# A two-layer diffusion backbone on one core: operands at one address residue, a later spill, and conditioning sums finished in fours

## The chip, the cores and the metric

The kernel runs on one core of one Trainium2 chip. The metric is the device time of one execution in microseconds (us), the median of several runs. One further execution was recorded by the profiler; its times are the ones quoted from the trace.

The engines are TensorE (PE, with its weight loads PEld), VectorE (DVE), ScalarE (ACT), GpSimd (POOL) and SyncE (SP), whose queue issues nearly all DMAs of this kernel. SBUF has 128 partitions; all byte addresses below are addresses within a partition.

## The reference

512 latent tokens and 256 context tokens of width 1024 go through two layers. Layer 0 mixes tokens by centred mean pooling, layer 1 by grouped-query attention; each is followed by a squared-ReLU MLP of width 4096. Every sub-layer is normed before and after, and shift, scale and gate come from a conditioning vector by a linear map per layer:

```python
def ada_mods(cond, w, b):
    m = (jax.nn.silu(cond) @ w + b)[..., None, :]
    return jnp.split(m, N_MOD, axis=-1)

def sq_relu_mlp(h, w_in, w_out):
    return jnp.square(jax.nn.relu(h @ w_in)) @ w_out

def reference(x, c, ctx, c_ctx, ...):
    for i in range(DEPTH):
        last = i == DEPTH - 1
        sh1, sc1, gt1, sh2, sc2, gt2 = ada_mods(c, w_ada[i], b_ada[i])
        csh1, csc1, cgt1, csh2, csc2, cgt2 = ada_mods(c_ctx, w_ada[i], b_ada[i])
        h_lat = modulate(rms_norm(x, g_mix_pre[i]), sh1, sc1)
        ...
        x = x + gt1 * rms_norm(y_lat, g_mix_post[i])
        m_lat = sq_relu_mlp(modulate(rms_norm(x, g_mlp_pre[i]), sh2, sc2), w_mlp_in[i], w_mlp_out[i])
        x = x + gt2 * rms_norm(m_lat, g_mlp_post[i])
        if not last:
            ...
    return x
```

The context stream gets the same in layer 0, with the conditioning vector `c_ctx`; in layer 1 it serves only as keys and values. So the six modulation vectors of layer 0 and `SH1`, `SC1` of layer 1 are needed for two conditioning vectors, the others of layer 1 for one. All is in float32.

## The kernel before

**Split matmuls.** Each float32 operand is kept as two parts of a faster matmul format, `hi` (a rounded copy) and `lo` (the rest). A product is three matmuls: hi·hi + hi·lo + lo·hi. So every weight tile that lands from HBM (1 MB, 128 x 2048, a tile `raw`) is split: ScalarE copies `hi` (L120), VectorE subtracts to get `lo` (L123). `Ring.load` does the load and the split.

**Where the operands lie.** `ra` (normed activations for the input matmuls), `rb` (hidden activations and others) and the three slots `unit` for split weights are the operands of nearly all matmuls. `unit[0]` is a part of `rb` at first; `unit[1]` and `unit[2]` are the tile `units`, which is allocated after a small tile `phase` of 24 floats. Its start, 124768, is 352 modulo 512; `ra` and `rb` start at 416 modulo 512. The tile `sums` starts at 157600, 416 modulo 512, over the memory of the residual `xr`, which starts at 157632; so `xr` is spilled to DRAM before `sums` is written, and loaded again after the first MLP.

**Stages.** The start (0 to 110 us) loads inputs and layer 0's conditioning weights and does the pooling mixer. Then come the first MLP (110 to 610), norms and QKV (610 to 733), attention (733 to 830), its output product (830 to 909) and the second MLP (909 to 1248).

**The first MLP** goes over 16 groups g of 256 hidden columns with all 768 tokens. Group 0 is done by `Inner` (L526); from group 1 on, `Seven` (L636) does the input product of a group with seven half-size products instead of eight. For this `sums` holds sums of activations, and `weights_sums` makes sums of weights, with short VectorE steps of 128 x 512 (L610 to L615) and splits of 128 x 1024 (L602, L603). `out_mm` (L731) does the output product of a group; its moving operand is `w_out`, split in `unit[2]`, and `out_ev` (L740, L742) adds the result into `acc`. The weight buffers `raw` are three, shared with the conditioning weights. **The second MLP** does the same for 512 tokens without `Seven`; its weights go through four slots in turn, two in `units` and two in `ra`.

**Conditioning.** A unit is one 256-column piece of a modulation vector of layer i. The first 20 units (layer 0, all but `GT2`) are computed on TensorE at the start (`ada_mm`, L212, and `ada_sel`, L219). The other 28 run on VectorE during the first MLP, by `ada_sum`: the piece of `w_ada` is loaded, eight passes over 128 x 256 multiply it by the conditioning vector and add up (L246, L251; twice eight for two vectors), a transpose (L254) and a reduction (L256) into a small tile `part` follow. `ada_fin` then spreads the sums over the partitions by small matmuls (L219) and adds the bias (L229). `ada_step` is called twice in each group, by `extra0` before the group's input product and by `mid0` ahead of its seventh product: each call finishes the unit of one group before and sums a new one. Twelve units have two vectors, sixteen have one.

**What sets the order.** Code of the start, of the last group and of attention goes into a `Steps` object, `st.at(t, f, ...)`, which sorts it by hand-written due times. After that the framework's scheduler sets the order on each engine by its own estimate of time, except for what `keep_in_program_order` pins. So the order on an engine can change at places that the code leaves alone.

The allocations that fix the places are these:

```python
ra = const.tile([P, 2 * KT * TOK], F32R, name="ra")
rb = const.tile([P, 10240], F32R, name="rb")
phase = ctx.enter_context(tc.tile_pool(name="phase", bufs=1)).tile([P, 24], F32, name="phase")
...
units = ctx.enter_context(tc.tile_pool(name="units", bufs=1)).tile([P, 2 * 4096], F32R, name="units")
```

## Time and profile before

| | us |
|---|---|
| median of 3 runs | 1252.26 (1252.23 to 1252.82) |
| the profiled execution | 1250.13 |
| its span in the trace, first to last instruction | 1248.2 |
| busy: TensorE matmuls | 1191.6 |
| busy: VectorE | 923.5 |
| busy: ScalarE | 524.6 |
| mean granted TensorE clock | 0.985 |

Lines of the profile have the form "start, duration, engine, tiles, line, count" in the chain of waits (the chain of work that ended last, followed back from the end) and in the timeline. In the timeline and the wait rows the square bracket names the idle time before an instruction and what ended it, and `x24` says that 24 like instructions are joined in a row. A group row gives after the bar the total busy time and the mean in ns of one, then the idle time before the group. Matmuls are pipelined, so the mean of one (some 390 ns) is longer than the distance from one to the next (some 230 ns). A window row gives the stretch, its length, then for PE, PEld, DVE, ACT and POOL the busy time with the count, the granted clock, the share of DMA and its GB/s.

### The profile page before, as it was taken

To read this page: it belongs to the slowest core of one execution; us is meant where nothing else is said; L and a number is where in the kernel's file an instruction comes from. 1 tells how busy PE (TensorE), PEld (TensorE's weight loads), DVE (VectorE), ACT (ScalarE), POOL (GpSimd) and SP (SyncE) were. 2 spreads that over 40 slices of the span, in tenths; PEclk is the share of its full clock that TensorE was granted. 3 is DMA by queue.
4 is the path that set the end of the run, shared out by engine and by line. 5 is a ranking of instruction groups with operands and counts; after the bars stand their busy time and mean duration, and the time that the engine had idled before them with its cause. 6 is when DMAs were issued, how large, how long until landed. Compare 5 with 4: busy or idle time off the path is not lost.

```text
span 1248.2 us, 16629 instructions
## 1 busy us (share of the span) xinstructions
PE 1191.6 (95%) x6602; PEld 1017.9 (82%) x6602; DVE 923.5 (74%) x1546; ACT 524.6 (42%) x868; POOL 101.8 (8%) x135
## 2 busy tenths in 40 slices
PE   6889989999999999999999989999999999999997
PEld 5669878888888888888787879988878888888886
DVE  3877998999898999987687589872664554555555
ACT  5666313433333333333476358862632222313222
POOL 1060000000000000000242232001100000000001
PEclk9899989999999999999999989999999999999999
DMA  9985044444444444343521211020233242333201
GB/s 330 345 296 177 1 139 131 135 135 135 136 135 135 135 133 138 124 128 122 198 72 54 82 34 35 1 81 21 68 119 117 70 133 68 103 100 96 73 1 68
DMA packets 105006, 143.71 MB, mean 115 GB/s; under 512 B 2608, under 2 KB 88032, under 8 KB 104928
## 3 DMA queue, kind: packets, MB, share of 16 engines
q1 hardware_dynamic: 104928, 142.64, 35.0%
q8 instruction: 52, 0.85, 0.3%
q14 instruction: 26, 0.21, 0.1%
HBM read 137.39 MB, written 5.24 MB: 114 GB/s over the span
## 4 chain that ended last, share of the span: by engine, by line
PE 78%; DVE 9%; DMA 6%; ACT 3%; issue 1%; POOL 1%; SPq 1%; DVEq 0%; POOLq 0%; ACTq 0%
PE pso L731 30%; PE psin L636 16%; PE psin L526 14%; PE psq L851 5%; DMA raw<-in_w_ada 4%; PE psy L1090 3%; PE po L1064 3%; PE pss L1025 2%; DMA raw<-in_w_mlp_in 2%; PE pspt L1050 1%; ACT junk L146 1%; PE pspool L454 1%; DVE xr L310 1%; PE psada L212 1%; DVE units L123 1%
## 5 line engine op out<-in xcount | busy, mean ns | idle before, releaser
L731 PE MATMUL pso<-units,rb 128*128 128x512 f32 x1542 | 376.6, 396 | 1.9 <-DVE units L123 1.7
L731 PEld LDWEIGHTS pso<-units,rb 128*128 128x128 f32 x1542 | 289.2, 189 | 66.4 <-DVE units L123 2.0
L742 DVE TENSOR_TENSOR acc<-acc,pso 128x512 f32<-128x512 f32 (+1 forms) x281 | 183.7, 680 | 107.2 <-PE pso L731 107.1
L120 ACT CAST units<-raw 128x2048 fp32r<-128x2048 f32 (+1 forms) x46 | 72.7, 1597 | 116.8 <-PE pso L731 95.5
L251 DVE SCALAR_TENSOR_TENSOR rows<-raw,cond,rows 128x256 f32<-128x256 f32 x280 | 117.1, 480 | 0.0
L123 DVE TENSOR_TENSOR units<-raw,units 128x2048 fp32r<-128x2048 f32 (+1 forms) x44 | 86.2, 1972 | 28.1 <-ACT units L120 28.1
L731 PE MATMUL pso<-ra,rb 128*128 128x512 f32 (+1 forms) x390 | 91.1, 386 | 0.0
L157 POOL TENSOR_SCALAR ms<-ss 128x1 f32<-128x1 f32 x21 | 10.5, 502 | 973.2 <-ACT junk L146 972.6
L526 PE MATMUL psin<-ra,units 128*128 128x512 f32 (+1 forms) x320 | 87.5, 375 | 0.0
L731 PEld LDWEIGHTS pso<-ra,rb 128*128 128x128 f32 x390 | 72.6, 188 | 15.2
L526 PE MATMUL psin<-ra 128*128 128x512 f32 x256 | 80.3, 390 | 0.0
L120 ACT CAST ra<-raw 128x2048 fp32r<-128x2048 f32 x16 | 30.4, 1906 | 108.6 <-PE pso L731 82.8
L636 PE MATMUL psin<-ra,units 128*128 128x384 f32 x336 | 66.2, 342 | 1.2 <-ACT psin L648 0.6
L526 PEld LDWEIGHTS psin<-ra,units 128*128 128x128 f32 x320 | 58.7, 188 | 9.3
L636 PE MATMUL psin<-sums,units 128*128 128x384 f32 x336 | 65.4, 342 | 0.5 <-ACT psin L644 0.3
L636 PEld LDWEIGHTS psin<-ra,units 128*128 128x128 f32 x336 | 58.0, 188 | 4.7 <-ACT psin L648 3.2
L636 PEld LDWEIGHTS psin<-sums,units 128*128 128x128 f32 x336 | 57.7, 188 | 3.0 <-ACT psin L644 1.8
L526 PEld LDWEIGHTS psin<-ra 128*128 128x128 f32 x256 | 48.1, 188 | 10.3
L123 DVE TENSOR_TENSOR ra<-raw,ra 128x2048 fp32r<-128x2048 f32 x16 | 36.6, 2291 | 25.2 <-ACT ra L120 25.2
L851 PE MATMUL psq<-units,ra 128*128 128x512 f32 x216 | 53.0, 397 | 0.0
L659 ACT ACTIVATE work<-work 128x768 f32<-128x768 f32 x14 | 11.9, 847 | 91.5 <-DVE work L654 91.5
L526 PE MATMUL psin<-rb,ra 128*128 128x512 f32 x128 | 49.9, 390 | 0.0
(214 smaller groups left out, 2045.5 us busy)
## 6 DMA issues: line engine op xcount, KB each, us to landing
raw<-in_w_ada SPq DMA_DIRECT2D x48, 1024.0 KB, 7.7
raw<-in_w_mlp_in SPq DMA_DIRECT2D x32, 1024.0 KB, 5.5
raw<-in_w_mlp_out SPq DMA_DIRECT2D x32, 1024.0 KB, 5.0
raw<-in_w_qkv SPq DMA_DIRECT2D x6, 1024.0 KB, 5.3
raw<-in_w_o SPq DMA_DIRECT2D x4, 1024.0 KB, 5.1
spill<-xr SPq DMA_DIRECT2D x6, 512.0 KB, 10.5
xr<-spill SPq DMA_DIRECT2D x6, 512.0 KB, 6.9
xr<-in_x SPq DMA_DIRECT2D x4, 512.0 KB, 4.5
```

Of the source, the lines that this page charges most:

```text
L120: a = gp.tensor_copy(hi, raw) if pool_hi else sc.copy(hi, raw)
L123: b = (gp if pool_lo else ve).tensor_tensor(out=lo, in0=raw, in1=hi, op=ALU.subtract)
L146: sc.activation(junk[:, 0:src.shape[-1]], src, AF.Square, scale=float(D) ** -0.5, accum_out=ss)
L251: ve.scalar_tensor_tensor(out=r, in0=raw[:, k, :], scalar=cond[:, k, c:c + 1], in1=r, op0=ALU.mult, op1=ALU.add)
L526: te.matmul(ps[:, bank, o:o + ln], w[:, k, fs], rhs, start=(k == 0 and n == 0), stop=(k == KT - 1 and n == 2))
L636: te.matmul(bank, w[k], a[k], start=start and k == 0 and m == 0, stop=stop and k == 3 and m == 2, skip_group_check=True)
L731: te.matmul(pss[h][:, 0:cols[h][1]], a[:, f, ts_], w[:, f, cols[h][0]:sum(cols[h])], start=(n == 0), stop=(n == len(seq) - 1))
L742: ve.tensor_tensor(out=d, in0=d, in1=ps[:, 0:w], op=ALU.add)
L851: te.matmul(ps, a[:, k, sl], w[:, k % 4, :], start=(k == 0 and n == 0), stop=(k == KT - 1 and n == 2))
L1025: te.matmul(ps[:, c2, 0:384], a[:, sl], b[:, kv, 384 * c2:384 * c2 + 384], start=(n == 0), stop=(n == 2))
L1064: te.matmul(po[:, 0:256], v[:, kt, hs], p[:, kt, qs], start=(kt == 0 and n == 0), stop=(kt == NT - 1 and n == 2))
L1090: te.matmul(ps, a[:, k, sl], w[:, k % 4, o:o + width], start=(k == 0 and n == 0), stop=(k == KT - 1 and n == 2))
```

## The change

1. `phase` grows from 24 to 40 floats, 64 bytes. `units` then starts at 124832, 416 modulo 512, and so do all the matmul operands named above.
2. The six spills of the residual are issued in `sums()`, in program order behind group 1's `w_in` and group 0's `w_out`, instead of at due times in the start.
3. `ada_sum` writes its reduction into a tile `parts` of 192 floats, cut off the end of `sums`. `ada_fin` finishes the four units of one modulation vector at a time (four matmuls, one bias step), three steps after the fourth sum. No unit runs in group 0; 24 units run in groups 1 to 12, one with two vectors and one with one vector in each.
4. The four units of (layer 1, `GT2`) are summed in groups 4 to 7 of the second MLP and finished in its group 10; there `gate_diag` follows, which stood in the attention's output stage.
5. In the first MLP the weights that `Ring.load` splits are split in two halves of 1024 columns each.

```diff
-    phase = ctx.enter_context(tc.tile_pool(name="phase", bufs=1)).tile([P, 24], F32, name="phase")
+    phase = ctx.enter_context(tc.tile_pool(name="phase", bufs=1)).tile([P, 40], F32, name="phase")
...
+    def split_halves(raw, hi, lo):
+        for q in range(2):
+            z = slice(1024 * q, 1024 * q + 1024)
+            sc.copy(hi[:, z], raw[:, z])
+            ve.tensor_tensor(out=lo[:, z], in0=raw[:, z], in1=hi[:, z], op=ALU.subtract)
...
-            if wait is None:
+            if wait is None and self.halves:
+                split_halves(raw, hi, lo)
+            elif wait is None:
                 split(raw, hi, lo, pin)
...
-        s = small.tile([P, 2, 8], F32, tag="part", name="part", bufs=2)
-        ve.tensor_reduce(out=s[:, 0:nc_, :], in_=raw[:, 0:nc_, :].rearrange("p c (g q) -> p c g q", q=32),
-                         axis=AX.X, op=ALU.add)
-        rowsd[i, m, j] = s, nc_
-
-    def ada_fin(i, m, j):
-        part, nc_ = rowsd.pop((i, m, j))
+        ve.tensor_reduce(out=part.rearrange("p (c g) -> p c g", c=nc_),
+                         in_=raw[:, 0:nc_, :].rearrange("p c (g q) -> p c g q", q=32), axis=AX.X, op=ALU.add)
+
+    def ada_fin(i, m, parts, nc_):
+        n = 4 * nc_
         ps = psB.tile([P, 512], F32, tag="b", name="psada")
-        ada_turn(ps[:, 0:2 * nc_], part[:, 0:nc_, :].rearrange("p c (b a) -> p a c b", a=4), nc_)
-        ada_out(i, m, j, ps[:, 0:2 * nc_], nc_)
+        for a in range(4):
+            te.matmul(ps[32 * a:32 * a + 32, 0:2 * n], sel,
+                      parts.rearrange("p (u c b a) -> p a u b c", c=nc_, b=2, a=4)[:, a], start=True, stop=True)
+        ada_out(i, m, 0, ps[:, 0:2 * n], nc_, 8)
...
     def sums():
+        for t in (4, 5, 0, 1, 2, 3):
+            sy.dma_start(spill[:, t], xr[:, t])
         held.close()
...
-        f = S["held"].enter_context(tc.tile_pool(name="sums", bufs=1, side="right")).tile([P, 8712], F32R, name="sums")[:, 0:8704]
+        pool = S["held"].enter_context(tc.tile_pool(name="sums", bufs=1, side="right"))
+        f, parts[0] = pool.tile([P, 8520], F32R, name="sums"), pool.tile([P, 192], F32, name="parts")
...
-        st.at([61.98, 66.18, 70.38, 74.58, 78.78, 82.98][n], lambda t: sy.dma_start(spill[:, t], xr[:, t]), t)
...
-            one = lambda z: Ring([z])
+            one = lambda z: Ring([z], True)
...
-    def ada_step(slot, kinds):
-        for u in due[slot]:
-            ada_fin(*u[:3])
-        due[slot] = [kinds.pop(0)] if kinds else []
-        for u in due[slot]:
-            ada_sum(*u)
+    dual = [(0, GT2, 2), (1, SC1, 2), (1, SH1, 2)]
+    lone = [(1, m, 1) for m in (GT1, SC2, SH2)]
+    work, due = [], []
+    for n in range(12):
+        work.append((*dual[n // 4], n % 4, 64 * (n // 4 % 2)))
+        work.append((*lone[n // 4], n % 4, 128 + 32 * (n // 4 % 2)))
+
+    def ada_step():
+        for u in [u for u in due if u[0] <= 0]:
+            ada_fin(*u[1:])
+        due[:] = [(u[0] - 1, *u[1:]) for u in due if u[0] > 0]
+        if work:
+            i, m, nc_, j, at = work.pop(0)
+            ada_sum(i, m, j, nc_, parts[0][:, at + 8 * nc_ * j:at + 8 * nc_ * j + 8 * nc_])
+            if j == 3:
+                due.append((2, i, m, parts[0][:, at:at + 32 * nc_], nc_))
...
     def mid0(g):
-        ada_step(1, lone)
+        if g:
+            ada_step()
...
-        ada_step(0, dual or lone)
-        if g == NG - 2:
-            ada_step(1, [])
+        if g:
+            ada_step()
...
-        at(36, gate_diag, 1, GT2, 0, 1)
...
+    def extra1(g):
+        if g == 3:
+            slot[0:NL] = [1] * NL
+            parts[1] = small.tile([P, 32], F32, tag="part", name="part", bufs=1)
+        if 3 < g < 8:
+            ada_sum(1, GT2, g - 4, 1, parts[1][:, 8 * g - 32:8 * g - 24])
+        if g == 10:
+            ada_fin(1, GT2, parts[1], 1)
+            gate_diag(1, GT2, 0, 1)
```

**The DMA queue of SP in the start.** The first fence is the queue before, from the load of group 0's `w_in` (`raw<-in_w_mlp_in`) on; `in_w_ada` are conditioning weights, `spill<-xr` the spills.

```order
L106 DMA raw<-in_w_mlp_in 128x8x256
L703 DMA spill<-xr 128x1024
L106 DMA raw<-in_w_ada 128x8x256 x2
L703 DMA spill<-xr 128x1024
L106 DMA raw<-in_w_ada 128x8x256 x2
L703 DMA spill<-xr 128x1024
L106 DMA raw<-in_w_ada 128x8x256
L703 DMA spill<-xr 128x1024 x3
L106 DMA raw<-in_w_mlp_in 128x8x256
L106 DMA raw<-in_w_mlp_out 128x2x1024
L106 DMA raw<-in_w_ada 128x8x256 x2
```

The same stretch after the change:

```order
L106 DMA raw<-in_w_mlp_in 128x8x256
L106 DMA raw<-in_w_ada 128x8x256 x4
L571 DMA spill<-xr 128x1024 x2
L106 DMA raw<-in_w_ada 128x8x256
L571 DMA spill<-xr 128x1024 x3
L106 DMA raw<-in_w_mlp_in 128x8x256
L106 DMA raw<-in_w_mlp_out 128x2x1024
L571 DMA spill<-xr 128x1024
L106 DMA raw<-in_w_mlp_out 128x2x1024
L106 DMA raw<-in_w_mlp_in 128x8x256
L106 DMA raw<-in_w_ada 128x8x256 x2
```

Four of the five conditioning loads now stand ahead of every spill, the last spill stands behind the next two MLP weights, and the first conditioning loads of the MLP stand behind group 1's weights.

**TensorE between groups 0 and 1.** The 96 matmuls are the last of group 0's input product; `pso` is the output product, `psada` a finish of a conditioning unit, and `psin` of 128x384 behind it the products of `Seven`. Before:

```order
L526 MATMUL psin<-ra,units 128x384 x96
L731 MATMUL pso<-units,rb 128x512 x72
L219 MATMUL psada<-part,sel 32x2x2 x4
L219 MATMUL psada<-part,sel 32x2 x4
L731 MATMUL pso<-units,rb 128x512 x18
L636 MATMUL psin<-ra,units 128x384 x2
L731 MATMUL pso<-units,rb 128x512 x5
L636 MATMUL psin<-ra,units 128x384 x10
```

After:

```order
L534 MATMUL psin<-ra,units 128x384 x96
L741 MATMUL pso<-units,rb 128x512 x24
L647 MATMUL psin<-ra,units 128x384 x12
L741 MATMUL pso<-units,rb 128x512 x51
L647 MATMUL psin<-sums,units 128x384 x4
L741 MATMUL pso<-units,rb 128x512 x21
L647 MATMUL psin<-sums,units 128x384 x20
```

The two finishes between the output matmuls of groups 0 and 1 are gone, and 12 matmuls of the next input product stand among the 72 of group 0.

**VectorE ahead of the split of group 1's `w_out`** (`units<-raw,units`). `rows<-raw,cond,rows` is a pass of a conditioning sum, `acc<-pso` an evacuation of an output product, `work<-raw` a short step of the weights' sums. Before:

```order
L740 COPY acc<-pso 128x512
L251 SCALAR_TENSOR_TENSOR rows<-raw,cond,rows 128x256 x2
L740 COPY acc<-pso 128x512
L251 SCALAR_TENSOR_TENSOR rows<-raw,cond,rows 128x256
L740 COPY acc<-pso 128x512
L251 SCALAR_TENSOR_TENSOR rows<-raw,cond,rows 128x256 x3
L123 TENSOR_TENSOR units<-raw,units 128x2048
```

After:

```order
L626 TENSOR_TENSOR work<-raw,work 128x512
L121 TENSOR_TENSOR units<-raw,units 128x1024
L259 SCALAR_TENSOR_TENSOR rows<-raw,cond,rows 128x256
L121 TENSOR_TENSOR units<-raw,units 128x1024
L259 SCALAR_TENSOR_TENSOR rows<-raw,cond,rows 128x256
L614 TENSOR_TENSOR units<-work,units 128x1024
```

The split is now two halves, with short steps of the weights' sums ahead of it where passes of the conditioning sums stood.

More of the change, by code (lines that the diff above doesn't have):

```diff
@@ L129, in backbone, with __init__ @@
     class Ring:
-        def __init__(self, slots):
-            self.slots, self.n = slots, 0
+        def __init__(self, slots, halves=False):
+            self.slots, self.n, self.halves = slots, 0, halves
         def load(self, src, width, pin=False, wait=None):
@@ L225, in ada_sel, with ada_out @@
         ada_out(i, m, j, ps[:, 256:260], 2)
-    def ada_out(i, m, j, ps, nc_):
+    def ada_out(i, m, j, ps, nc_, w=2):
         at = m * KT + 2 * j
-        ve.tensor_tensor(out=mods[i][:, at:at + 2, 0:nc_], in0=ps.rearrange("p (b c) -> p b c", c=nc_),
-                         in1=cols[:, i * 48 + at: i * 48 + at + 2].unsqueeze(2).broadcast_to([P, 2, nc_]),
+        ve.tensor_tensor(out=mods[i][:, at:at + w, 0:nc_], in0=ps.rearrange("p (b c) -> p b c", c=nc_),
+                         in1=cols[:, i * 48 + at: i * 48 + at + w].unsqueeze(2).broadcast_to([P, w, nc_]),
                          op=ALU.add)
@@ L234, in ada_out, with ada_sum @@
             g0 = 96 + s * 16 + i * KT + 2 * j
-            ve.scalar_tensor_tensor(out=avec[i][s][:, 2 * j:2 * j + 2, 0:nc_], in0=mods[i][:, at:at + 2, 0:nc_],
+            ve.scalar_tensor_tensor(out=avec[i][s][:, 2 * j:2 * j + w, 0:nc_], in0=mods[i][:, at:at + w, 0:nc_],
                                     scalar=1.0,
-                                    in1=cols[:, g0:g0 + 2].unsqueeze(2).broadcast_to([P, 2, nc_]),
+                                    in1=cols[:, g0:g0 + w].unsqueeze(2).broadcast_to([P, w, nc_]),
                                     op0=ALU.add, op1=ALU.mult)
-    def ada_sum(i, m, j, nc_):
+    def ada_sum(i, m, j, nc_, part):
         raw = raw_load(w_ada[i, :, m * D + j * 256: m * D + (j + 1) * 256]
```

7 lines of the change are left out of this document (2 added, 5 removed).

## The prediction

> **What bounds the kernel now.** I read the head of the page first, then the windows by stage, the chain of work that ended last, and the timelines of the places that the change touches.
>
> ```profile
> PE 1191.6 (95%) x6602; PEld 1017.9 (82%) x6602; DVE 923.5 (74%) x1546; ACT 524.6 (42%) x868; POOL 101.8 (8%) x135
> PE 78%; DVE 9%; DMA 6%; ACT 3%; issue 1%; POOL 1%; SPq 1%; DVEq 0%; POOLq 0%; ACTq 0%
> 228.30:293.30 65.00, 64.85 (x351) 56.49 (x345) 61.19 (x121) 23.97 (x31) 0.00 (x0) 1.00 0.41 130
> 909.00:1219.00 310.00, 308.22 (x1344) 251.75 (x1343) 171.43 (x197) 86.76 (x86) 0.00 (x0) 1.00 0.27 89
> ```
>
> TensorE is busy 95% of the span and holds 78% of the chain. In the second MLP (909 to 1219 us) it is the only bound: 308 of 310 us busy, VectorE 171. In the first MLP (the window at 228 us holds two of its groups g) TensorE is as full, but VectorE has 61.2 of 65.0 us, so it stands close behind. Two groups seen along the chain:
>
> ```profile
> 358.54 0.17 PE psada L219 x8
> 358.72 0.55 PE psin L636 x2
> 359.27 0.17 PE psada L219 x8
> 359.44 2.28 PE psin L636 x12
> ...
> 378.01 2.10 PE psin L636 x12
> ...
> 380.75 0.61 DVE part L256
> 381.36 0.02 issue
> 381.37 5.56 DMA raw<-in_w_mlp_in
> ...
> 392.66 1.15 DVE units L603
> 393.81 0.04 issue
> 393.85 2.00 PE psin L636 x10
> ```
>
> The chain leaves TensorE once: a conditioning sum ends (L256), its buffer goes to the next weights, these land 5.56 us later, and their split ends when TensorE needs it. So here two limits are in balance.
>
> **A. Operands at 416 modulo 512 bytes.** Of the matmul operands only `units` starts at 352; `ra`, `rb` and `sums` start at 416. The second MLP reads its moving operand from `units` and from `ra` in turn:
>
> ```profile
> 986.94 5.60 PE pso L731 x24
> 998.91 5.44 PE pso L731 x24
> L731 PE MATMUL pso<-units,rb 128*128 128x512 f32 x1530 | 374.8, 397 | 1.9 <-DVE units L123 1.7
> L731 PE MATMUL pso<-ra,rb 128*128 128x512 f32 x378 | 89.3, 390 | 0.0
> L851 PE MATMUL psq<-units,ra 128*128 128x512 f32 x216 | 53.0, 397 | 0.0
> L526 PE MATMUL psin<-rb,ra 128*128 128x512 f32 x128 | 49.9, 390 | 0.0
> 68.04 2.86 PE pspool L454 x24
> 754.90 2.13 PE po L1064 x18
> ```
>
> The first chain row streams from `units`, 233 ns from matmul to matmul; the second from `ra`, 227 ns. The means per matmul agree: 397 from `units`, 390 from `ra` and from `rb`, which lies elsewhere at the same residue. With 512 columns 1530 + 216 = 1746 matmuls stream from `units` (the 72 of `psy` are left out): 1746 x 6 ns = 10.5 us. With 256 columns the sign may turn: `po` from `units` goes at 118 ns (2.13 / 18), `pspool` from `rb` at 119 (2.86 / 24); 288 of `po` lose 0.3 us. Matmuls that load the stationary operand from `units` I leave at no change. After the first MLP's last group the path runs through normalisations in part, so I book **-10** (bounds: 0, if the residue is not the cause, and -11). The Trainium skill, "TensorE: Matmul & The Clock Gate", section "Back-to-back issue gap", gives N/2.4 + 2.5 ns for an isolated warm matmul, some 216 ns for 512 columns, with no term for the address; the rows show 233 and 227. By that rule A would be 0.
>
> **B. Spill later.** The DMA queue of SP now stands still for up to 10.3 us ahead of a spill, which waits for a residual (total, times and longest wait in the first row; the second counts TensorE's waits for conditioning weights from 60 to 115 us):
>
> ```profile
> SPq L703 <- DVE xr L310: 15.2, 2, 10.3
> PE psada L212 <- DMA raw<-in_w_ada: 4.4, 3, 2.3
> 90.55 1.28 DVE L310 SCALAR_TENSOR_TENSOR xr<-acc,rs,xr 128x1024 f32<-128x1024 f32 x1 [0.44 <-POOL rs L159]
> spill<-xr SPq DMA_DIRECT2D x6, 512.0 KB, 10.5
> 123.50 0.84 ACT L583 CAST sums<-work 128x768 fp32r<-128x768 f32 x1 [1.33 <-DVE work L581]
> ```
>
> After the change four loads stand ahead of any spill. They need a free buffer, but not the residual, so they can go up to 10.3 us earlier. TensorE waits 4.4 us for such loads, in three places. Next late is the last residual (90.55 to 91.83), held partly by the same loads, and behind it the norms of the last pairs on VectorE and ScalarE. I book **-3.5** (0 to -6). The `sums` tile lies over the residual, so its first write now waits for the last spill. That spill stands behind two weight loads; issued at some 95 us it lands 10.5 us later (the median), at 105.5, and the first write to `sums` is at 123.5 us. Some 18 us of cover make this free.
>
> **C. No conditioning unit in group 0.** TensorE now stands still before group 1:
>
> ```profile
> 161.68 0.61 PE L219 MATMUL psada<-part,sel 128*32 128x4 f32 x16 [7.87 <-DVE part L256]
> 119.64 0.96 DVE L542 TENSOR_TENSOR work<-work 128x768 f32<-128x768 f32 x1 [4.45 <-ACT work L535]
> 155.78 2.29 DVE L123 TENSOR_TENSOR units<-raw,units 128x2048 fp32r<-128x2048 f32 x1
> L251 DVE SCALAR_TENSOR_TENSOR rows<-raw,cond,rows 128x256 f32<-128x256 f32 x280 | 117.1, 480 | 0.0
> L603 DVE TENSOR_TENSOR units<-raw,units 128x1024 fp32r<-128x1024 f32 x14 | 17.1, 1220 | 0.3 <-ACT units L602 0.3
> ```
>
> That stall of 7.87 us goes, since the finishing instruction is no longer there. But VectorE runs without a break from 119.64 to the split at 155.78 and is next late. By the order its list up to that split loses five multiply-adds and one multiplication (0.48 us each) and gains a split of 1024 columns (1.22 us) and five short steps of group 1's weights (0.69, the rows under "what VectorE gives back"): 1.22 + 5 x 0.69 - 6 x 0.48 = 1.8 us. So the first half of the `w_out` split ends near 155.8 + 1.8 + 1.2 = 158.8 us. Group 1's output matmuls could then start 3.4 us earlier than 161.7 + 0.6 = 162.3, and 12 matmuls of group 1 (2.1 us) are done in the gap. I book **-5** (-2 to -9).
>
> **D. Finishing in fours.** 224 `psada` matmuls from `part` (28 units of 8) become 7 sets of 8. In the chain above two finishes cost 2 x 0.17, and each makes the matmuls behind it start late (0.55 for 2 instead of 0.35, 2.28 for 12 instead of 2.10): 0.73, or 0.37 each. 26 lie outside group 0's stall: 9.6 us. The seven sets are wider; at 0.4 each they cost 2.8. **-6.8** (-9 to -3).
>
> **What VectorE gives back.**
>
> ```profile
> 386.96 0.69 DVE L610 TENSOR_TENSOR work<-raw 128x512 f32<-128x512 f32 x1 [1.72 <-DMA raw<-in_w_mlp_in]
> 420.71 0.69 DVE L610 TENSOR_TENSOR work<-raw 128x512 f32<-128x512 f32 x1 [0.70 <-DMA raw<-in_w_mlp_in]
> ```
>
> Two groups now take some 65 us. TensorE would need 2.1 less (144 x 6 ns, and three finishes). VectorE's 61.2 lose some 0.6 (the small steps of the finishes) and gain 0.3 (below), and its waits for the weights' DMA, 1.72 and 0.70 us in these two groups, don't depend on TensorE: 61.2 - 0.3 + 2.4 = 63.3 in all, so 1.8 of the 2.1 is to be had, and a little less where the order is worse. Over twelve groups **+2.5** (0 to +13).
>
> **Halved splits, and what moves to the second MLP.**
>
> ```profile
> L120 ACT CAST units<-raw 128x2048 fp32r<-128x2048 f32 x35 | 66.6, 1905 | 116.8 <-PE pso L731 95.5 <-PE psin L526 19.1 <-PE psq L851 2.0
> L602 ACT CAST units<-raw 128x1024 fp32r<-128x1024 f32 x14 | 14.7, 1051 | 45.5 <-DMA raw<-in_w_mlp_in 45.5
> ```
>
> A split in two halves costs ScalarE 2 x 1051 - 1905 = 197 ns and VectorE 2 x 1.22 - 2.29 = 0.15 us more. ScalarE has room (24 of 65 us), VectorE's 0.3 per two groups stands above; the split begins when the first half of the old weights has been read. Net **0** (-1 to +2.5). Four single units go to the second MLP: some 4.5 us of VectorE each (eight passes of 0.48, a transpose, a reduction) beside 171 of 310 us busy, and 1 MB each where the DMA share is 0.27. Each adds a load to the three weight buffers, and the next `w_in` waits for its sum. That is hidden while a weight load lands before its split; if that cover went, one load of 5.56 us would be bare, four times. The matmuls of the gate's `diag` only change place. **0** (-1 to +6).
>
> **Sum.** -10 - 3.5 - 5 - 6.8 + 2.5 = -22.8 us. The profiled execution took 1250.13 us (its span is 1248.2), so 1227.3; the median of the runs stands 2.13 above it at 1252.26, so I predict **1229.5**.
>
> **The rivals.**
> 1. *The 6 ns belong to the place of `units`, not to its residue.* All of `units` is one stretch of memory, so the trace cannot split the two. Against it: `rb` and `ra` lie 49 KB apart and agree. A falls to 0, and the give-back shrinks to 0.5, since TensorE asks for less: -14.8, **1237.5**. The page of the Trainium skill named under A gives this result too.
> 2. *VectorE becomes the bound of the first MLP.* For it: 61.2 of 65.0 us. Then A's part there (1152 matmuls, 6.9 us) and D's 6.8 stay out of reach: -22.8 + 13.7 - 2.5 = -11.6, **1240.7**.
> 3. *Slower: weights behind sums.* The load of `w_in` waits for the buffer of the two-column sum, and the rows 381.37 to 393.85 show no slack behind it. If the new order ends that sum later by one single-column sum's passes (8 x 0.48 = 3.8 us) in every second group, six times 3.8 = 23 us come on top of case 2: **1264**. It turns the sign from 11.6 / 6 = 1.9 us on. Against it: the order keeps two units per group and the same sequence of loads.
> 4. *The spills don't get out of the way*, because the four loads wait for their buffers and not for the spill. B is 0: **1233**, inside the forecast's own range.
>
> **How the numbers follow.** Forecast with case 4: 0.65, between 1216 and 1239 (bounds of B, C and D). Case 1: 0.14. Case 2: 0.13. Case 3: 0.06. The remaining 0.02 is left to a mixture that ends within 0.2% of before. The range from 1214 to 1246 holds the forecast and cases 1 and 2 with the bounds of their terms, and leaves out case 3 and the ends. A measurement of this kernel can tell about 0.2% (2.5 us) from no change. Case 2 lies 11.6 us under before; I give 0.01 of it to within. Faster by more: 0.65 + 0.14 + 0.12 = 0.91; within: 0.01 + 0.02 = 0.03; slower: 0.06.
>
> **What would show it.** A: in the second MLP 24 matmuls from `units` take 5.45 us as those from `ra` do; if they still take 5.60, case 1 holds. B: no wait of SP for L310 ahead of the conditioning loads, and TensorE without the 4.4 us of waits for `in_w_ada` before 115 us. C: no wait of 7.9 us on `part`, and group 1 starts 4 to 9 us earlier. D: 56 `psada` matmuls from the sums, and two groups in 63 to 63.5 us. If two groups still take 65 us with VectorE over 62, case 2 holds; if `psin` waits for splits behind late `w_in` loads, case 3. Wrong altogether would be a second MLP that is longer than 310 us.

## The result, and the profile after

The changed kernel takes 1229.62 us (median of 4 runs, 1228.51 to 1231.44), the kernel before beside it 1252.24: a ratio of 0.9822, with a 95% interval from 0.9805 to 0.9839. The forecast was 1229.5. The profiled execution took 1229.90 us, its span is 1227.8. The profiled execution of before, at 1250.13 us, was 2.1 us under its median, so the traces show some 2 us less of a gain than the medians.

The total came out as forecast; its terms did not. The first rows are the head of the page after, then windows of the first MLP from group 2 on (186 to 570 us) and of the second MLP from its first input matmul (861 us; before, that stands at 879 us). The last row is the first MLP before, groups 2 to 13:

```profile
PE 1176.2 (96%) x6434; PEld 1015.4 (83%) x6434; DVE 928.5 (76%) x1536; ACT 525.5 (43%) x885; POOL 103.1 (8%) x135
186.00:570.00 384.00, 377.38 (x1890) 333.09 (x1889) 348.72 (x646) 140.66 (x189) 0.00 (x0) 1.00 0.40 129
861.00:1221.00 360.00, 355.14 (x1626) 295.52 (x1624) 222.94 (x287) 109.19 (x127) 4.91 (x12) 1.00 0.29 98
```

```profile
203.00:605.00 402.00, 398.38 (x2119) 348.34 (x2118) 362.49 (x675) 149.43 (x191) 0.00 (x0) 1.00 0.42 134
```

In the first MLP TensorE now stands still for 6.6 of 384 us (busy 98%), with VectorE 91% busy (348.72 of 384). Before, TensorE was busy 99% and VectorE 90%. What TensorE was given there it does not fully use. The second MLP is nearly all TensorE. The chain of work that ended last carries less than before:

```profile
PE 40%; DVE 3%; issue 3%; ACT 2%; POOL 2%; POOLq 0%; DVEq 0%; ACTq 0%
```

Its shares add up to half of the span, since it breaks off near the end of the first MLP (its first pieces stand at some 607 us); where a chain does that, it says nothing of what lies ahead of its start, and other views have to be read there.

To place the gain I read the start times of single matmuls in the traces. Five marks serve for all kernels below: the first input matmul of group 0, the first output matmul of group 1, the last output matmul of the first MLP, the first of attention's output product (`psy`), and the last matmul.

| us | group 0 in | group 1 out | MLP 0 ends | `psy` | last |
|---|---|---|---|---|---|
| before | 97.0 | 162.2 | 640.6 | 832.2 | 1240.9 |
| after | 89.8 | 148.9 | 621.4 | 815.3 | 1220.5 |
| difference | -7.2 | -13.3 | -19.2 | -16.9 | -20.5 |

So 7.2 us come from the start, 12.0 from the first MLP, then 2.3 are lost up to `psy` and 3.6 gained behind it. The first MLP's 12.0 can be split further. Undisturbed, a matmul of 512 columns starts 227 ns after the one before, 384 columns take 173, 256 columns 119. With these distances the matmuls from the last 96 of group 0's input product to the end of the first MLP take 489.7 us before and 486.0 after (fewer finishes). The 6 ns of `units` come to 6.9 us before and nothing after. The rest is TensorE standing still or going slowly: 23.7 before, 22.3 after. Its place has moved, though: 8.2 us lay between groups 0 and 1 before and 0.9 after, and from group 2 to 14 it was 12.5 before and is 19.3 after.

The start of group 1, before (two windows, then TensorE's timeline) and after (TensorE's timeline):

```profile
156.00:168.00 12.00, 6.28 (x31) 4.95 (x32) 10.42 (x20) 2.61 (x3) 0.00 (x0) 0.57 0.73 232
162.00:168.00 6.00, 6.00 (x23) 4.75 (x24) 4.47 (x9) 2.61 (x3) 0.00 (x0) 0.58 1.02 329
162.22 6.67 PE L731 MATMUL pso<-units,rb 128*128 128x512 f32 x18
```

```profile
137.40 11.08 PE L741 MATMUL pso<-units,rb 128*128 128x512 f32 x48
148.94 0.96 PE L741 MATMUL pso<-units,rb 128*128 128x512 f32 x3 [0.46 <-ACT units L120]
150.84 0.97 PE L647 MATMUL psin<-sums,units 128*128 128x384 f32 x4 [0.94 <-ACT units L613]
```

The wait of 7.87 us is gone, and with it its second price: behind it the granted clock was 0.58, and 18 matmuls took 6.67 us, 370 ns each instead of 233. Waits of 0.5 and 0.9 us are left, behind which the clock stays at 1.00 here.

Short waits can lower the clock all the same. In the changed kernel TensorE waits for 0.63, 0.23 and 0.64 us within 3 us. In the kernel "all at 480" below, which has the same order of instructions, these waits are 0.47, 0.23 and 0.63 us. The window behind them and the 12 matmuls in it, in the changed kernel and then at 480:

```profile
374.50:377.90 3.40, 3.03 (x7) 2.45 (x8) 3.40 (x6) 1.04 (x1) 0.00 (x0) 0.50 0.00 0
374.87 4.39 PE L741 MATMUL pso<-units,rb 128*128 128x512 f32 x12 [0.64 <-DVE units L121]
```

```profile
374.50:377.90 3.40, 3.09 (x14) 2.58 (x15) 3.40 (x6) 1.05 (x1) 0.00 (x0) 1.00 0.00 0
374.81 3.03 PE L741 MATMUL pso<-units,rb 128*128 128x512 f32 x12 [0.63 <-DVE units L121]
```

One execution has such a stretch of 3.4 us at half clock, the other has none: 1.4 us for these 12 matmuls. The changed kernel's trace has two more that some of the traces below lack, at 644 and 873 us, which cost 1.4 and 1.5 us. They are in its marks, and other traces have theirs at other places, so I name them where they bear on a difference.

### The profile page after: what moved, and what is told of

Same layout as the page of the kernel before. It is cut to its first block, busy times and chain, and to the rows that moved or that the text cites. A ratio compares the mean times of both kernels' runs of the same rounds, so it can differ in the third digit from the quotient of the medians.

```text
span 1227.8 us, 16301 instructions
## 1 busy us (share of the span) xinstructions
PE 1176.2 (96%) x6434; PEld 1015.4 (83%) x6434; DVE 928.5 (76%) x1536; ACT 525.5 (43%) x885; POOL 103.1 (8%) x135
## 4 chain that ended last, share of the span: by engine, by line
PE 40%; DVE 3%; issue 3%; ACT 2%; POOL 2%; POOLq 0%; DVEq 0%; ACTq 0%
PE pso L741 14%; PE psin L534 14%; PE psy L1106 3%; PE po L1080 3%; PE pss L1041 2%; PE psq L867 2%; PE pspt L1066 1%; ACT junk L154 1%; DVE xr L318 1%; POOL rs L876 1%; DVE work L892 0%; POOL ms L165 0%; POOL rs L167 0%; PE psx L343 0%; DVE units L1069 0%
## 5 line engine op out<-in xcount | busy, mean ns | idle before, releaser
L741 PE MATMUL pso<-units,rb 128*128 128x512 f32 x1542 | 370.6, 392 | 4.2 <-DVE units L121 1.3
L259 DVE SCALAR_TENSOR_TENSOR rows<-raw,cond,rows 128x256 f32<-128x256 f32 x280 | 125.8, 486 | 1.2
L165 POOL TENSOR_SCALAR ms<-ss 128x1 f32<-128x1 f32 x21 | 11.1, 527 | 952.3 <-ACT junk L154 951.6
L126 ACT CAST units<-raw 128x2048 fp32r<-128x2048 f32 (+1 forms) x29 | 40.3, 1417 | 93.6 <-PE pso L741 76.5
L126 ACT CAST ra<-raw 128x2048 fp32r<-128x2048 f32 x16 | 30.4, 1908 | 95.8 <-PE pso L741 68.4
L647 PE MATMUL psin<-sums,units 128*128 128x384 f32 x336 | 63.5, 337 | 1.6 <-ACT units L613 1.4
L129 DVE TENSOR_TENSOR units<-raw,units 128x2048 fp32r<-128x2048 f32 (+1 forms) x27 | 47.8, 1797 | 19.2 <-ACT units L126 19.2
L129 DVE TENSOR_TENSOR ra<-raw,ra 128x2048 fp32r<-128x2048 f32 x16 | 36.6, 2292 | 24.0 <-ACT ra L126 24.0
L867 PEld LDWEIGHTS psq<-units,ra 128*128 128x128 f32 x216 | 40.2, 188 | 8.2
```

The costliest lines, as they stand in the source:

```text
L126: a = gp.tensor_copy(hi, raw) if pool_hi else sc.copy(hi, raw)
L129: b = (gp if pool_lo else ve).tensor_tensor(out=lo, in0=raw, in1=hi, op=ALU.subtract)
L259: ve.scalar_tensor_tensor(out=r, in0=raw[:, k, :], scalar=cond[:, k, c:c + 1], in1=r, op0=ALU.mult, op1=ALU.add)
L647: te.matmul(bank, w[k], a[k], start=start and k == 0 and m == 0, stop=stop and k == 3 and m == 2, skip_group_check=True)
L741: te.matmul(pss[h][:, 0:cols[h][1]], a[:, f, ts_], w[:, f, cols[h][0]:sum(cols[h])], start=(n == 0), stop=(n == len(seq) - 1))
L867: te.matmul(ps, a[:, k, sl], w[:, k % 4, :], start=(k == 0 and n == 0), stop=(k == KT - 1 and n == 2))
```

## The experiments

Twelve kernels: three make one part of the change in the kernel before, six undo one part in the changed kernel, three measure something else. Times are medians; the ratio is to runs of the kernel before on the same chip.

| kernel | time, us | ratio (95%) | group 0 in | group 1 out | MLP 0 ends | `psy` | last |
|---|---|---|---|---|---|---|---|
| before + alignment | 1244.43 | 0.9939 (0.9928 to 0.9951) | 97.1 | 162.3 | 637.2 | 829.5 | 1235.7 |
| before + later spill | 1252.01 | 0.9995 (0.9985 to 1.0005) | 89.4 | 155.0 | 641.8 | 834.9 | 1243.0 |
| before + no unit in group 0 | 1261.83 | 1.0081 (1.0066 to 1.0097) | 97.9 | 158.8 | 651.8 | 846.8 | 1254.9 |
| after, 352 again | 1232.59 | 0.9853 (0.9836 to 0.9869) | 89.3 | 148.8 | 622.6 | 815.4 | 1223.3 |
| after, early spill | 1234.08 | 0.9863 (0.9847 to 0.9879) | 97.0 | 155.7 | 626.1 | 820.6 | 1224.2 |
| after, units in group 0 | 1234.02 | 0.9854 (0.9830 to 0.9879) | 89.4 | 146.4 | 626.6 | 819.1 | 1224.3 |
| after, single finishes | 1233.31 | 0.9863 (0.9844 to 0.9882) | 89.6 | 148.6 | 625.5 | 818.1 | 1222.9 |
| after, whole splits | 1236.42 | 0.9878 (0.9856 to 0.9900) | 90.4 | 150.7 | 631.9 | 824.3 | 1229.1 |
| after, four units kept | 1243.82 | 0.9939 (0.9917 to 0.9961) | 89.0 | 148.7 | 632.0 | 822.8 | 1231.2 |
| after, fewer passes | 1216.67 | 0.9719 (0.9699 to 0.9739) | 89.7 | 148.8 | 608.7 | 803.3 | 1208.2 |
| after, first product on ScalarE | 1218.56 | 0.9732 (0.9712 to 0.9751) | 90.3 | 149.4 | 610.0 | 805.9 | 1210.7 |
| after, all at 480 | 1227.22 (one run) | | 89.4 | 148.5 | 619.8 | 814.2 | 1217.9 |

The intervals are some 2 us wide on either side, so differences of 3 to 4 us between two variants of the changed kernel are at the edge of what the times show. The differences of times that I give for them are up to 1.4 us smaller and 0.4 us larger than those of the ratios, which allow for the chip. For such differences I look at the marks too. The granted clock is part of the spread: four units kept, for instance, took 1240.5 us in the run with a mean clock of 0.994 and 1246.4 in that with 0.989.

**Alignment, alone and undone.** The order of instructions stays that of before and of after.

```diff
-.tile([P, 24], F32, name="phase")
+.tile([P, 40], F32, name="phase")
```

> The kernel before with phase at 40 floats and nothing else; the order of instructions is that of before. Theory 1 (the prediction: a matmul that streams 512 columns from units costs 6 ns less wherever it stands): 233 ns become 227, and the time falls by about 10 us, to 1242. Theory 2 (the nanoseconds are real, but count only where TensorE is the bound): 233 become 227 in all stages, the second MLP falls by some 2.4 us, the first MLP by under 1.5 us, and the time by 3 to 4 us, to about 1249. Theory 3 (it is the place of units, not its residue): 233 ns stay and the time stays within 1 us of before.

The second kernel has the reverse edit in the changed kernel:

> The changed kernel with phase back at 24 floats; the order of instructions is that of the changed kernel. Theory 1: slower by about 10 us (less some give-back in the first MLP, 8 at least), 1238 to 1240. Theory 2: slower by 3 to 4 us, about 1233, of it 2.4 in the second MLP and under 1.5 in the first. Theory 3: within 1 us of the changed kernel.

The groups of TensorE that stream 512 columns from `units`: alignment alone, the changed kernel, the changed kernel at 352, then at 480 (below):

```profile
L731 PE MATMUL pso<-units,rb 128*128 128x512 f32 x1530 | 369.3, 394 | 1.8 <-DVE units L123 1.7
L741 PE MATMUL pso<-units,rb 128*128 128x512 f32 x1530 | 368.8, 393 | 4.2 <-DVE units L121 1.3 <-ACT units L120 1.2 <-DVE units L129 1.2
L741 PE MATMUL pso<-units,rb 128*128 128x512 f32 x1530 | 374.1, 396 | 3.8 <-DVE units L121 1.1 <-DVE units L129 1.1 <-ACT units L120 1.0
L741 PE MATMUL pso<-units,rb 128*128 128x512 f32 x1530 | 367.4, 392 | 4.2 <-DVE units L121 1.3 <-DVE units L129 1.2 <-ACT units L120 1.1
```

The mean falls from 397 to 393 or 394, the median distance from start to start from 233 to 227 ns. Theory 3 falls. By the times it is worth 7.6 us in the kernel before (ratio; 5.2 by the marks) and 3.0 in the changed one (3.9 by the ratios, 2.8 by the marks). The two sizes can't be told apart, though, since the clock differs. The changed kernel's four runs had a mean clock of 0.988 to 0.990. With 352 again three had 0.993 to 0.995 (1232.5 to 1232.6 us), and the one at 0.989 took 1236.5 us, 7 us more than the changed kernel. In the kernel before the first MLP gets 3.4 us shorter, of 6.9 that its matmuls save; in the changed one 1.75 (from the last 96 matmuls of group 0 to its end), and some 3.2 without the stretch at 374 us, which the trace at 352 lacks. The second MLP gets 2.3 and 2.5 us shorter; its 378 matmuls x 6 ns are 2.3. But both aligned traces have a stretch at half clock in it, 1.5 us each, that the trace at 352 beside them lacks, so the saving is nearer 4 us; part of the rest lies in input products whose stationary operand is in `units`. The chain shows the 6 ns in the second MLP, in the changed kernel and with 352 again:

```profile
958.11 5.44 PE pso L741 x24
968.09 5.44 PE pso L741 x24
...
990.07 5.44 PE pso L741 x24
1001.63 5.44 PE pso L741 x24
```

```profile
957.72 5.60 PE pso L741 x24
967.87 5.60 PE pso L741 x24
...
990.08 5.44 PE pso L741 x24
1001.70 5.60 PE pso L741 x24
```

With 352 the rows that stream from `units` take 5.60 us and those from `ra` 5.44; at a shared residue all take 5.44. In the kernel before the time (1244.4 us) lies between theory 1 (1242) and theory 2 (1249), nearer to theory 1. In the changed kernel the median is that of theory 2 (1233) and the run at equal clock (1236.5 us) is nearer to theory 1 (1238 to 1240).

**Shared residue, or 416?** The three tiles and `sums` move by 64 bytes; to make room the small tile `phase0` goes.

```diff
+    pad = const.tile([P, 16], F32, name="pad")
     ra = const.tile([P, 2 * KT * TOK], F32R, name="ra")
```

> The changed kernel with ra, rb, units and sums all moved from 416 to 480 modulo 512 (a pad of 16 floats ahead of ra); the order of instructions is that of the changed kernel. If what counts is that both operands of a matmul share a residue, matmuls that stream 512 columns from units stay at 227 ns and the second MLP is as long as in the changed kernel, within 0.5 us. If 416 is special, they rise to 230 ns or more, and those from ra and rb with them: the second MLP would be 4 us longer or more.

The distance stays 227 ns. The second MLP takes 358.0 us, against 359.5 in the changed kernel's trace with the stretch at 873 us; the changed kernel with early spills, which has the residue 416 and no such stretch, takes 358.0 as well. In the kernel that keeps the four units (below) `units` happens to start at 288, and there it is 233 ns on average, as at 352. So 416 is nothing special: in these four layouts what counts is that both operands share the residue.

**Later spill, alone and undone.**

```diff
     def sums():
+        for t in (4, 5, 0, 1, 2, 3):
+            sy.dma_start(spill[:, t], xr[:, t])
...
-        st.at([61.98, 66.18, 70.38, 74.58, 78.78, 82.98][n], lambda t: sy.dma_start(spill[:, t], xr[:, t]), t)
```

> The kernel before with the six spills issued in sums() and nothing else. Prediction: 3.5 us less, about 1248.8, since three waits of 4.4 us in all for conditioning weights go. Theory from the trace of after: the first input matmul of group 0 starts near 90 us instead of 97.0, because the low granted clock behind these waits goes too, and the time falls by about 7 us, to 1245; what the scheduler reorders in the first MLP may add or take some us behind that point. Rival (the earlier start came from the conditioning loads that group 0 no longer has): first input matmul at 96 to 97 us, time unchanged.

The reverse edit in the changed kernel:

> The changed kernel with the spills back at their due times in the start. Prediction for part B: +3.5 us, 1233. Theory 2 (the start's gain is 7 us wherever it is made, but in the kernel before the first MLP gave it back in groups 8 to 14, where VectorE was late): first input matmul of group 0 near 97 instead of 89.8, and +3 to +7 us at the end, since the changed kernel's VectorE has more room. Rival (given back here too, as in the kernel before): within 1.5 us of the changed kernel at the end.

TensorE's longest waits in the start, with the spills late (alone in the kernel before), and with the spills early in the changed kernel:

```profile
PE psin L526 <- DVE ra L350: 1.7, 2, 0.9
PE psada L219 <- DVE rows L214: 0.7, 1, 0.7
```

```profile
PE psada L220 <- DMA raw<-in_w_ada: 5.1, 2, 3.3
PE psin L534 <- DVE ra L358: 1.6, 1, 1.6
```

Both kernels agree on the start: the waits for conditioning weights go and group 0 starts 7.2 to 7.6 us earlier, twice the forecast's 3.5. They part behind it. In the kernel before, the gain is still 8.0 us at group 8 and all gone at group 14, so the time doesn't change. In the changed kernel 4.7 of 7.2 us are left at the end of the first MLP, and 4.5 us in the time; 1.4 us of what is missing is the stretch at 374 us, which the trace with early spills lacks. In the kernel before the loss lies between groups 8 and 14, where TensorE waits for splits of `w_out` in an order that the scheduler has changed:

```profile
PE pso L732 <- DVE units L123: 3.5, 3, 1.3
PE pso L732 <- ACT units L120: 2.4, 2, 1.2
```

**No unit in group 0, alone and undone.**

```diff
     def mid0(g):
-        ada_step(1, lone)
+        if g:
+            ada_step(1, lone)
```

The same `if g:` stands before the step in `extra0`; the last two units are finished before `sums` is released.

> The kernel before with no conditioning unit in group 0; the 28 units run in groups 1 to 14 and are finished one by one, the last two after group 14. Prediction for part C: 5 us less, about 1247. Theory from the trace of after: the wait of 7.9 us for part goes, and with it the matmuls at half clock behind it (18 in 6.67 us instead of 4.1), less what VectorE is late: 7 to 9 us less by the start of group 2, about 1244 if nothing is given back later. Rival (the units only move, and a first MLP bound by VectorE gets them back): under 3 us less.

In the changed kernel the two `if g:` are taken out:

> The changed kernel with its conditioning units in groups 0 to 11 instead of 1 to 12, still finished in fours. Prediction for part C: +5 us, 1234.6, lost before group 1's output matmuls, which would start some 3 to 8 us later than at 148.9 us. Theory 2: the wait of 7.9 us belonged to the finish, which is no longer there, so the start of group 1 loses at most 3 us and groups 12 and 13, which no longer have a unit, give back as much: within 2 us of the changed kernel at the end of the first MLP.

Alone, the part makes the kernel 10 us slower (ratio 1.0081). Group 1 starts 3.5 us earlier, as forecast, but with 28 units in groups 1 to 14 TensorE waits for VectorE and ScalarE, and 14.7 us are lost between there and the end of the first MLP. Some 5.6 us of them, worked out from the distances of the matmuls, go to three stretches behind such waits, 13.7 us in all, in which the granted clock was 0.50 (at 359, 557 and 611 us). Undone in the changed kernel it costs 4.4 us by the time, the size of the forecast, but not at its place: group 1 starts 2.5 us earlier, without the wait of 7.9, and the loss comes from the end of group 1 on. Neither expectation had that. The wait belonged to the finishing instruction, and with finishing in fours it is gone whether or not group 0 has units.

**Finishing in fours, undone.**

```diff
-            if j == 3:
-                due.append((2, i, m, parts[0][:, at:at + 32 * nc_], nc_))
+            due.append((1, i, m, parts[0][:, at + 8 * nc_ * j:at + 8 * nc_ * j + 8 * nc_], nc_, j, 1))
```

> The changed kernel with each of the 24 units of the first MLP finished by itself, two steps after its sum. Prediction for part D: 18 finishes more at 0.37 each are 6.7 us, less what VectorE gives back (0.5 to 1): about +6, 1235.5. Theory 2 (TensorE has slack in the first MLP of the changed kernel, since it waits there for split weights, so part of a finish is hidden): +1 to +4, 1231 to 1233.5.

The time is 3.7 us higher (5.1 by the ratios, 2.5 by the last mark, 4.1 at the end of the first MLP). That is nearer to theory 2 than to the forecast's 6 us, but the intervals don't exclude the forecast.

**Halved splits, undone.**

```diff
-            one = lambda z: Ring([z], True)
+            one = lambda z: Ring([z])
```

> The changed kernel with whole splits of 2048 columns in the first MLP. Prediction: halves are worth 0 (-1 to +2.5), so 1229.6 within 1 us, and 0.15 us of VectorE per split is saved. Theory 2: with the finishes gone the split of w_out is what the output matmuls of a group wait for, and the half lets them start a good 1 us earlier; without halves the start of a group waits more often, +2 to +5 us, and the first MLP's idle time of TensorE grows by as much.

The time is 6.8 us higher, more than both expectations. TensorE's waits from 186 us on, in the first MLP, that name a whole split (L126 copies, L129 subtracts):

```profile
PE pso L741 <- ACT units L126: 3.5, 2, 1.8
PE pso L741 <- DVE units L129: 1.6, 2, 1.3
```

They come to 5.1 us. In the changed kernel those for the halves (L120, L121) come to 2.0:

```profile
PE pso L741 <- DVE units L121: 1.3, 3, 0.6
PE pso L741 <- ACT units L120: 0.7, 2, 0.5
```

With the start of group 1 counted in (112 us on) the two sums are 7.9 and 2.5 us. So the split does limit the start of a group's output product, and a half lets it start earlier. The rest lies behind the waits, in the clock of the kernel with whole splits:

```profile
152.10:158.90 6.80, 5.91 (x15) 4.34 (x14) 6.76 (x10) 0.40 (x1) 0.00 (x0) 0.50 0.87 309
315.90:322.70 6.80, 5.64 (x13) 4.46 (x14) 6.80 (x10) 2.10 (x2) 0.00 (x0) 0.50 1.05 341
350.10:353.40 3.30, 2.94 (x9) 2.95 (x10) 3.09 (x8) 2.31 (x3) 0.00 (x0) 0.50 0.72 218
```

These 17 us at half clock, against 3.4 in the first MLP of the changed kernel, cost some 5 us more by the distances of the matmuls (an estimate from the trace). With the 5.4 us of waits that accounts for the 9.9 us by which this first MLP is longer. The profiled execution was the longest of the four, 1238.5 us at a mean clock of 0.984; the one at 0.991 took 1232.8. The scheduler also puts other instructions in another order, which this run does not separate.

**Four units kept in the first MLP.**

```diff
-    lone = [(1, m, 1) for m in (GT1, SC2, SH2)]
+    lone = [(1, m, 1) for m in (GT1, SC2, SH2, GT2)]
...
+        if g == NG - 2:
+            ada_step()
```

> The changed kernel with the four units of (layer 1, GT2) summed in groups 13 and 14 of the first MLP (28 units in groups 1 to 14) and finished after it; the gate's matmuls stay in the second MLP. Prediction: the move is worth 0 (-6 to +1), so 1229.6 to 1230.6, or less. Theory V: four sums of some 4.5 us on VectorE and four more weight loads come back into groups 13 and 14, which have no room: +8 to +12 us, 1238 to 1242, all of it between groups 8 and 15 of the first MLP, while the second MLP gets shorter by less than 1 us.

The time is 14.2 us higher. Up to group 12 the kernel runs level with the changed one (output product of group 12 at 507.8 and 507.6 us), at group 14 it is 9.9 us behind. Without the tile `part` of the second MLP `units` starts at 288, so I put the 2.8 us that it loses in the second MLP down to the 6 ns again (2.5 us with 352) and not to the move. Two windows of groups 11 to 14, kept and moved:

```profile
480.00:587.00 107.00, 101.86 (x508) 89.74 (x507) 98.10 (x182) 38.97 (x53) 0.00 (x0) 0.98 0.44 145
480.00:587.00 107.00, 106.01 (x545) 94.97 (x544) 90.30 (x152) 43.25 (x60) 0.00 (x0) 1.00 0.40 130
```

VectorE has 98.1 us of work there instead of 90.3, and TensorE does 37 matmuls less in the same time. Its longest wait there is for split sums of the next weights, which VectorE makes:

```profile
PE psin L647 <- DVE units L614: 4.1, 2, 2.9
```

**Is it VectorE or the loads?** 84 of the 280 passes are left out; the loads stay.

```diff
-        for k in range(1, KT):
+        for k in range(1, 1 if nc_ == 1 and m != GT2 else KT):
```

> The changed kernel, leaving out 7 of the 8 passes of the twelve one-vector sums in the first MLP (these sums then cover one eighth of their columns); all weights are still loaded, and the order of the DMAs is the same. VectorE does 84 passes of some 0.4 us less, 34 us. Theory V (VectorE sets the pace of the first MLP from group 2 to 14, where TensorE's matmuls stand 19 us further apart than their undisturbed distance): -8 to -15 us, about 1218. Rival (the loads of weights and their three buffers set it): -3 us or less.

The time falls by 13.0 us. The same stretch as in the second row of the result, without the passes and then with the first product on ScalarE (below):

```profile
186.00:570.00 384.00, 383.39 (x1956) 344.92 (x1955) 325.66 (x570) 146.48 (x196) 0.00 (x0) 1.00 0.40 129
186.00:570.00 384.00, 382.86 (x1951) 344.28 (x1950) 346.16 (x617) 159.12 (x230) 0.00 (x0) 1.00 0.40 132
```

TensorE is busy 383.4 us instead of 377.4 with the same share of DMA (0.40), and does 66 matmuls more. So the loads are not the limit, and VectorE's sums are: theory V. A sum also holds its weight buffer until it ends; how much comes through the buffers that are free earlier, this run does not tell.

**A faster version: the first product on ScalarE.**

```diff
-            z = ve.tensor_scalar(out=r, in0=raw[:, 0, :], scalar1=cond[:, 0, c:c + 1], scalar2=None, op0=ALU.mult)
+            z = sc.activation(r, raw[:, 0, :], AF.Copy, scale=cond[:, 0, c:c + 1])
```

> The changed kernel with the first of the eight products of every sum on ScalarE (a scaled copy) instead of VectorE: 36 of them in the first MLP, some 0.35 us each, 12.6 us less on VectorE there. Theory V: leaving out 34 us of passes gave 13 us, so this gives 3 to 6, 1224 to 1227. Rival: ScalarE works in order, the product waits there behind copies that wait for TensorE, the sums end later and the weights behind them too: 0 to +5 us.

The products on ScalarE, of the faster version (40 in all, 36 of them in the first MLP):

```profile
L254 ACT ACTIVATE rows<-raw,cond 128x256 f32<-128x256 f32 x40 | 19.0, 503 | 4.5 <-DMA raw<-in_w_ada 4.3
```

1218.56 us, 11.1 less than the changed kernel and twice what I expected: nearly all that the left-out passes gave, for a third of their work. TensorE is busy 382.9 of 384 us, so from here on TensorE bounds the first MLP again, and what is taken from VectorE beyond this point gains little.

## Why the prediction came out right, point by point

The forecast hit the time by luck: its errors cancelled. The measured size of each part is what undoing it costs in the changed kernel; they add up to more than 22.6 us, since several parts make room for the same thing.

- **A (-10).** The mechanism holds: 233 ns become 227 at a shared residue, and the second MLP's 24 matmuls behave as the forecast said. The size is 3.0 us in the changed kernel by the medians (about 7 in the run at equal clock) and 7.6 in the one before. The step that failed priced all 1746 matmuls as if each stood on the path; in the first MLP 3.4 of 6.9 us arrive in the kernel before, and 1.75 in the changed one with its stretch at half clock. Of the rivals, case 1 (place, not residue) falls. The rule of the Trainium skill, "TensorE: Matmul & The Clock Gate", section "Back-to-back issue gap", by which A would be 0, has no term for addresses; the two distances speak against it here.
- **B (-3.5, 0 to -6).** The mechanism holds; the term is 7.2 us at the start of group 0 and 4.5 in the time. The step counted TensorE's waits for weights (4.4 us) and then cut them for "next late". Behind the waits stood a lowered clock that the step did not see, here in the window from 90 to 96 us, before and after:

```profile
90.00:96.00 6.00, 3.87 (x28) 2.64 (x28) 2.08 (x4) 1.71 (x3) 5.25 (x5) 0.72 0.94 330
```

```profile
90.00:96.00 6.00, 5.09 (x42) 4.70 (x41) 5.88 (x10) 6.00 (x13) 5.65 (x6) 1.00 1.03 376
```

  The granted clock is 0.72 there before and 1.00 after, and VectorE and ScalarE, at 2.08 and 1.71 of 6 us before, are full after. At 0.72 the clock costs at most 0.28 x 6 = 1.7 us, so with the waits of 4.4 us some 6 of the 7.2 us have a place; how they divide I did not test.
- **C (-5).** The size is right (4.4 us when undone), the mechanism is not. Group 1 starts 6.1 us earlier counted from group 0's start (13.3 - 7.2), but the wait went with the finish, so with part D. What the empty group 0 gives arrives later. As a single edit it is a loss of 10 us.
- **D (-6.8) and what VectorE gives back (+2.5).** Undoing D costs 3.7 us, against 6.8 forecast, or some 6 with D's part of the give-back. The give-back was mis-sized: TensorE's lost time from group 2 to 14 grew by 6.8 us (12.5 to 19.3), 1.4 of it the stretch at half clock. Two groups were to take 63 to 63.5 us; from group 2 to 12 they take 64.3 on average, and 64.6 before. The step that failed took VectorE's idle time in two quiet groups as free except for two waits. Case 2, given 0.13, describes the first MLP behind its start better than the forecast does: there A's part and D's are mostly not had.
- **Halves and the move (0 and 0).** These are the two large misses. Undoing the halves costs 6.8 us, keeping the four units 14.2 (some 10 without the shifted residue). The step that failed counted what four units cost in the second MLP (nothing, as it turned out) and never what they free in the first, though the same text had VectorE at 61.2 of 65 us and each unit at 4.5 us.
- **Sum.** By the medians A, D and the give-back fell short by some 14 us; B, the halves and the move made up for it.
- **Case 3 (weights behind sums)** did not come with the change; the slower kernels (no unit in group 0 alone, four units kept) show what more VectorE work in one stretch does: 10 and 14 us slower. **Case 4** falls, the spills did get out of the way.

What stays open: how much of the loss between groups 8 and 14 in single-edit kernels is work and how much is the order that the scheduler finds. No kernel pinned that order. Whether the change itself lowers the granted clock, through more short waits, or the runs happened to differ, is open as well. Norms, QKV and attention lose 2.3 us in the changed kernel: 0.9 of it is the dearer 256-column matmul below, and 1.4 is the stretch at half clock at 644 us, behind a wait of 3.1 us. With single finishes and with units in group 0 the same wait leaves the clock at 1.00, and this part takes 192.6 and 192.5 us; it takes 193.9 in the changed kernel and 191.7 before.

## What to carry to other kernels

When the bound engine and a second one are in balance, price each edit by what it frees on the second engine as well as by what it costs where it goes. Compare the granted clock before you compare two times: a stretch of 3.4 us at half clock, in one trace and not in the other, was as large as half of some terms here. The first MLP here paid almost one for one for VectorE time (12.6 us moved, 11.1 gained) until TensorE was full again. Parts of a change are not a sum: one of them alone was a loss of 10 us and inside the whole a gain of 4. A total that comes out right proves nothing about its terms; undo them one by one.

## What the runs showed of the hardware that was not expected

- Fp32r matmuls that stream 512 columns start 227 ns apart when streamed and stationary operand share their start modulo 512 bytes (416 with 416, 480 with 480) and 233 ns apart when the streamed one starts at 352 or 288 and the other at 416. With the roles exchanged the mean distance is 228 ns (352) and 233 (288). With 256 columns the sign turns: `po`, streamed from `units`, goes from 117 ns at 352 to 120 at 416.
- After a stall of 7.87 us the granted clock stood at 0.58 for a window of 6 us of full work, which made 18 matmuls 2.5 us longer than 18 x 233 ns. Stalls of 0.5 and 0.9 us left it at 1.00 in one place; behind three of 0.63, 0.23 and 0.64 us within 3 us it stood at 0.50 for 3.4 us in one execution, and behind nearly the same three at 1.00 in another. Behind a wait of 3.1 us in the QKV stage it was 0.50 in the changed kernel and 1.00 with single finishes and with units in group 0. The Trainium skill, "TensorE: Matmul & The Clock Gate", section "Why this matters for your kernels", warns of idle gaps above some 3 us; the stall of 7.87 us agrees, but the fall behind the three short waits goes beyond that rule, and here the measurement decides.
